# A streaming encoder step on one core: a fixed order for the beginning, token sums in place, the new stream read back from its sum in DRAM, pooling rows on the loads' queue, weight buffers moved

## The chip, the cores and the metric

The kernel runs on one core of a Trainium2 chip, as one launch. The metric is the device time of one execution in microseconds (us); of several runs the median is taken. Engines are named as in the profile: PE (TensorE, matmuls), DVE (VectorE), ACT (ScalarE), POOL (GpSimd, which also issues DMAs through a queue in software), SP (SyncE, which only issues DMAs).

## What is computed

A two-layer trunk over 640 tokens (512 of one prompt, and 8 running streams of 16), width 2048, in float32. Layer A, which the change touches:

```python
h = rmsnorm(x, norm_a[l])
z = h @ w_in_a[l]                       # 2048 -> 2 x 4096
u, gate = z[..., :E_A], z[..., E_A:]
y, st = pool_mix(u, pool_prev[l], pos0, w_grp_a[l], scale_a[l])
x = x + (y * jax.nn.silu(gate)) @ w_out_a[l]
new_pool.append(st)                     # the last 15 rows of u: outputs pool_prompt, pool_sample
```

`pool_mix` takes, for four groups of 1024 channels, the mean over a trailing window of 2, 4, 8 or 16 tokens minus the token, and multiplies each group by its own 1024 x 1024 matrix. Then the stream is normalised and projected once to keys and values (`w_kv`), and layer B attends over them. The outputs are the two streams, K, V, the forget logits and the pooling states.

## The kernel before, in words

Every float32 operand of a product is split into a high part (ACT's rounding copy, names ending in h or hi: `th`, `bh`, `wh`, `whi`) and the rest (a subtraction on DVE: `tl`, `bl`, `wl`, `wlo`), and a product is three matmuls: high by high, high by low, low by high (L242-246). A matmul is 128 x 128 by 128 x 320, since the 640 tokens are handled as two halves.

The large products of layer A are done in pairs, 256 rows by 256 columns at a time, by a scheme with seven products in place of eight (names m1 to m7, `OPER` at L124 says which operands each takes). For it a "side" of two token tiles holds three plain blocks (`bh`, `bl`, L160-163) and four sums of blocks (`th`, `tl`, L165-173). `blocks_t` takes the four sums from the four-block tile `x4` into another tile `t` (L167-170), then splits `t` (L172 on ACT, L173 on DVE). The weights have sums as well (`prep`, L204-226: L209, L212, L213 on DVE, in the last 16 preparations L212 and L213 on POOL; the splits at L86 and L89).

The work runs in this order:

1. The beginning (L322-384): five row tiles of x are loaded, squared (L352), normalised (L361), transposed by PE (L110) and copied into eight tiles `x4s` (L371, L373); from these come the eight sides. PE's first unit (L403) takes m1, m2, m3 of all sides, which need only `bh` and `bl`, and then m5, m6, m7, m4, which need `th` and `tl`.
2. Units u and g (`pair8`, L253): the pooling branch and the gate, 256 channels at a time. A u unit combines its products (L270-291), adds windows on POOL (L463) and stores the differences; its last 15 rows wait in a list of small pieces of work (`pool_rows`, L476), which later units run one at a time (`tick`): PE transposes them (L483), ACT copies them from PSUM (`po`, L485), POOL's queue stores them (L486). The tag `po` has one buffer. The saved states come in through `st` (L423-432).
3. For each of four groups g, four `y_pair` (group matrix, L543; scale and gate on DVE at L562 into `m4`) make the sides `y_[0..3]`, and eight `out_pair` (L567) multiply these by `w_out`, 256 rows of the stream each. In `out_pair` m1, m6, m5, m7 come first; ACT and DVE combine them (L581-585) and POOL's queue adds them to the stream in DRAM (`xacc`, accumulating DMA, L586). Then come m2, m3, m4. In groups 0 to 2 ACT copies these (L599) and two more accumulating DMAs add them (L600, L601). In group 3 SP reads the stream's rows back behind L586 (L589, into `x1`), DVE adds m2, m3, m4 to them (L605), POOL's queue stores the new stream (`xres`, L673), ACT squares it (L638), POOL adds up the squares (L640), and the first eight rows' tiles are split at once, the others later (`late`, L681).
4. The tail: the sum of squares goes to DRAM (`sqd`, L680), the pools of layer A are closed, the K/V weights are loaded into the space (L716), scaled (L722) and split (L730, L732), and PE projects (L701). A matmul with ones (L789) in the first projection, behind its first eight token tiles, sums the squares over partitions.

PE's order is that of the code (`manual_schedule`, L176); the other engines' orders are chosen by the scheduler, which may move an instruction ahead of older ones. DMAs of one queue are issued in order, and an instruction that waits holds up those behind it on its engine or queue. A DMA that writes rows which another DMA is writing waits until that one has landed.

Of the kernel before, what the change touches and what calls it, by code (L numbers as in the profile page):

```python
# [17 lines left out]
P = 128  # L18
# [21 lines left out]
def tile_yoco_step(ctx, tc, i, o):  # L40
# [36 lines left out]
    ident = const.tile([P, P], F32, name="ident")  # L77
    make_identity(nc, ident)
    inv = const.tile([P, 16], F32, name="inv")
    for t in range(16):  # L80
        nc.vector.memset(inv[:, t : t + 1], 1.0 / (t + 1))
# [42 lines left out]
    OPER = {"m1": (0, 0), "m6": (5, 5), "m5": (4, 3), "m7": (3, 4), "m2": (2, 2), "m3": (6, 1), "m4": (1, 6)}  # L124
# [12 lines left out]
    xb_, wa, misc = pool(sa, "xb"), pool(sa, "wa"), pool(sa, "misc")  # L137
# [27 lines left out]
    def blocks_t(sd, x4, t, eng=None):  # L165
        eng = eng or nc.vector
        eng.tensor_tensor(t[:, 0, :], x4[:, 0, :], x4[:, 1, :], op=ALU.subtract)  # L167
        eng.tensor_tensor(t[:, 1, :], x4[:, 2, :], x4[:, 0, :], op=ALU.add)
        eng.tensor_tensor(t[:, 2, :], x4[:, 2, :], t[:, 0, :], op=ALU.add)
        eng.tensor_tensor(t[:, 3, :], x4[:, 3, :], t[:, 2, :], op=ALU.subtract)  # L170
        sd.th, sd.tl = (tslot(sd.j, q, [P, 4, HALF], F32R) for q in "hl")
        nc.scalar.activation(sd.th, t, AF.Copy)  # L172
        nc.vector.tensor_tensor(sd.tl, t, sd.th.bitcast(F32), op=ALU.subtract)  # L173
# [30 lines left out]
    def prep():  # L204
        n = nprep[0]
        raw = loaded.pop(n).rearrange("p (a b) (s n) -> p a (b s) n", a=2, n=P)
        if loads[n][0] == "s":
# [3 lines left out]
            eng = nc.gpsimd if n >= len(loads) - 16 else nc.vector  # L211
            eng.tensor_tensor(sums[:, :, 2, :], sums[:, :, 1, :], raw[:, :, 1, :], op=ALU.add)  # L212
            eng.tensor_tensor(sums[:, :, 3, :], raw[:, :, 3, :], sums[:, :, 2, :], op=ALU.subtract)  # L213
# [56 lines left out]
    cvue = [misc.tile([P, HALF], F32, tag=f"c{q}", name=f"c{q}") for q in "vue"]  # L270
# [47 lines left out]
    gains = [bslot(6 + q // 2, "hl"[q % 2], [P, 512]) for q in range(4)]  # L318
    x4s = [tslot(4 + j // 2, "hl"[j % 2], [P, 4, HALF]) for j in range(8)]
    small = pool(start, "small")  # L320

    idle = small.tile([P, P], F32, name="idle")  # L322
    nc.vector.memset(idle, 0.0)
    for _ in range(8):
        nc.tensor.matmul(banks[:, 7, :P], idle, idle, start=True, stop=True)
# [4 lines left out]
    def half_rows(t):  # L330
# [4 lines left out]
    half_rows(0)  # L335
    for q in range(4):
        dma(gains[q], i["norm_a"][0][q * 512 : (q + 1) * 512].partition_broadcast(P))
# [975 lines left out]
```

## Time and profile before

| | |
|---|---|
| median of 3 runs | 2927.91 us (2926.19 to 2931.11) |
| the profiled execution | 2930.98 us |
| its span, first to last instruction | 2929.3 us |
| mean granted PE clock | 0.981 of full speed |
| PE busy | 2794.5 us, 95% |
| DVE, ACT, POOL busy | 66%, 35%, 13% |
| first unit's last products | until about 104 us |
| u and g units | until about 895 us |
| groups 0 to 3 | 895 to 1577.5 us |
| K/V projection begins | 1600.15 us |

A line of the waits reads "engine tile line <- engine tile line it waited for: us in total, times, longest us". In a timeline, a line has start, length, engine, line, operation, output and inputs; brackets at its end hold the idle time of the engine before it and what ended it. L numbers are lines of the kernel before; the lines of the changed kernel differ by up to some thirty.

### The profile page before, as it was taken

What the parts mean: (1) busy time and instruction counts of PE and PEld (TensorE: products, weight loads), DVE (VectorE), ACT (ScalarE), POOL (GpSimd) and SP (SyncE); (2) the same over time, 40 slices, a digit from 0 to 9 for tenths busy, and PEclk for the clock granted to TensorE, in tenths of its full rate; (3) what the DMA queues carried; (4) which work ended last, traced back from release to release, by engine and by line L of the source; (5) the groups of instructions that cost most, each with busy time, mean ns of one, the idle gap of its engine ahead of it and who ended that gap; (6) DMA issues with size and microseconds to landing.
All of it is one profiled execution on the core that took longest, in us unless ns stands there. A gap on an engine that the chain in (4) does not pass through costs nothing.

```text
span 2929.3 us, 46530 instructions
## 1 busy us (share of the span) xinstructions
PE 2794.5 (95%) x18410; PEld 2691.4 (92%) x18410; DVE 1935.2 (66%) x3350; ACT 1027.0 (35%) x1720; POOL 390.5 (13%) x426
## 2 busy tenths in 40 slices
PE   5899999999999999999986999999999999999998
PEld 4799999989999999999985999999999999999887
DVE  7777877787777848586674755655656666656434
ACT  6333333333334434343332232333333333334222
POOL 1312223133240110202244000000000000000000
PEclk9799999999999999999997999999999999999999
DMA  4344443433435786868466644455544455554823
GB/s 136 98 126 130 132 128 121 134 110 115 131 107 182 182 166 171 170 169 171 121 178 175 163 120 118 115 121 124 131 119 115 119 121 119 120 121 105 148 84 111
DMA packets 677643, 390.36 MB, mean 133 GB/s; under 512 B 323920, under 2 KB 632704, under 8 KB 677296
## 3 DMA queue, kind: packets, MB, share of 16 engines
q1 hardware_dynamic: 652256, 320.61, 41.3%
q0 software_dynamic: 25168, 66.78, 10.4%
q8 instruction: 144, 2.36, 0.3%
q14 instruction: 75, 0.61, 0.1%
HBM read 299.34 MB, written 87.95 MB: 132 GB/s over the span
## 4 chain that ended last, share of the span: by engine, by line
PE 42%; DMA 4%; DVE 1%; SPq 1%; POOL 1%; issue 1%; ACT 0%; DVEq 0%; POOLq 0%; ACTq 0%
PE banks L701 30%; PE banks L1205 5%; PE banks L1133 2%; DMA xacc<-m 2%; PE banks L1034 1%; DMA xt<-xres 1%; PE banks L110 1%; SPq L1243 1%; DMA x<-xacc 1%; POOL bh L640 1%; PE banks L1044 0%; PE banks L1045 0%; PE banks L1046 0%; DVE yn L1246 0%; PE banks L1146 0%
## 5 line engine op out<-in xcount | busy, mean ns | idle before, releaser
L246 PE MATMUL banks<-th,wh 128*128 128x320 f32 x1408 | 447.9, 318 | 12.6 <-ACT th L172 12.2
L246 PE MATMUL banks<-tl,wh 128*128 128x320 f32 x1408 | 442.9, 315 | 17.7 <-DVE tl L173 17.7
L246 PE MATMUL banks<-th,wl 128*128 128x320 f32 x1408 | 441.3, 313 | 0.0
L701 PE MATMUL banks<-th,whi 128*128 128x320 f32 x2048 | 399.6, 317 | 22.7 <-ACT whi L730 22.7
L701 PE MATMUL banks<-tl,whi 128*128 128x320 f32 x2048 | 384.0, 309 | 0.0
L246 PE MATMUL banks<-bh,wh 128*128 128x320 f32 x1056 | 332.8, 315 | 14.8 <-DVE x L605 9.8
L701 PEld LDWEIGHTS banks<-th,whi 128*128 128x128 f32 x2048 | 316.1, 189 | 29.0 <-ACT whi L730 23.0
L246 PE MATMUL banks<-bl,wh 128*128 128x320 f32 x1056 | 331.8, 314 | 3.1 <-DVE bl L163 3.1
L246 PE MATMUL banks<-bh,wl 128*128 128x320 f32 x1056 | 331.6, 314 | 0.6 <-DVE wl L89 0.6
L732 DVE TENSOR_TENSOR wlo<-raw,whi 128x512 fp32r<-128x512 f32 x272 | 186.3, 686 | 212.9 <-ACT whi L730 209.9
L701 PEld LDWEIGHTS banks<-tl,whi 128*128 128x128 f32 x2048 | 321.9, 188 | 0.0
L730 ACT ACTIVATE whi<-raw 128x512 fp32r<-128x512 f32 x272 | 171.7, 632 | 398.6 <-PE banks L701 234.3
L89 DVE TENSOR_TENSOR wl<-raw,wh 128x768 fp32r<-128x768 f32 (+1 forms) x200 | 209.4, 1048 | 142.5 <-ACT wh L86 136.3
L86 ACT ACTIVATE wh<-raw 128x768 fp32r<-128x768 f32 (+1 forms) x200 | 173.5, 869 | 342.8 <-issue 156.0
L246 PEld LDWEIGHTS banks<-tl,wh 128*128 128x128 f32 x1408 | 270.4, 192 | 20.9 <-DVE tl L173 20.9
L246 PEld LDWEIGHTS banks<-th,wh 128*128 128x128 f32 x1408 | 270.5, 192 | 17.2 <-ACT th L172 15.2
L246 PEld LDWEIGHTS banks<-th,wl 128*128 128x128 f32 x1408 | 270.0, 192 | 0.0
L89 DVE TENSOR_TENSOR wl<-sums,wh 128x1024 fp32r<-128x1024 f32 x176 | 223.6, 1271 | 42.5 <-ACT wh L86 41.9
L86 ACT ACTIVATE wh<-sums 128x1024 fp32r<-128x1024 f32 x176 | 185.2, 1052 | 188.6 <-DVE sums L213 183.4
L701 PE MATMUL banks<-th,wlo 128*128 128x320 f32 x1024 | 233.7, 309 | 0.2 <-DVE wlo L732 0.2
L701 PE MATMUL banks<-tl,wlo 128*128 128x320 f32 x1024 | 233.7, 309 | 0.0
L246 PEld LDWEIGHTS banks<-bh,wh 128*128 128x128 f32 x1056 | 203.3, 193 | 16.4 <-DVE x L605 10.3
(376 smaller groups left out, 5156.1 us busy)
## 6 DMA issues: line engine op xcount, KB each, us to landing
raw<-in_w_in_a SPq DMA_DIRECT2D x128, 512.0 KB, 4.0
raw<-in_w_out_a SPq DMA_DIRECT2D x64, 512.0 KB, 4.9
raw<-in_w_kv SPq DMA_DIRECT2D x128, 256.0 KB, 3.1
raw<-in_w_in_b SPq DMA_DIRECT2D x128, 256.0 KB, 3.0
raw<-in_w_grp_a SPq DMA_DIRECT2D x32, 512.0 KB, 5.6
kc<-in_cache_k SPq DMA_DIRECT2D x64, 256.0 KB, 4.1
vc<-in_cache_v SPq DMA_DIRECT2D x16, 1024.0 KB, 7.4
raw<-in_w_out_b SPq DMA_DIRECT2D x64, 256.0 KB, 3.2
```

The lines of the kernel that those rows point to most:

```text
L86: a = nc.scalar.activation(hi, x, AF.Copy)
L89: nc.vector.tensor_tensor(lo, x, hi.bitcast(F32), op=ALU.subtract)
L110: nc.tensor.transpose(out, x, ident[:n, :n])
L246: nc.tensor.matmul(bank[:, :HALF], w[kk][:, a, :], x, start=first and q == 0, stop=last and q == 2)
L640: nc.gpsimd.tensor_tensor(sqs[0], sqs[0], s, op=ALU.add)
L701: nc.tensor.matmul(acc_[:, s, :HALF], w, x[:, s * HALF : (s + 1) * HALF], start=f, stop=l)
L730: nc.scalar.activation(hi, raw, AF.Copy)
L732: nc.vector.tensor_tensor(lo, raw, hi.bitcast(F32), op=ALU.subtract)
L1034: nc.tensor.matmul(sp[rows, b % 2 * PAST : (b % 2 + 1) * PAST], qs[:, rows], kct[:, b * PAST : (b + 1) * PAST], start=True, stop=True)
L1133: nc.tensor.matmul(po[32 * q : 32 * q + 32, :P], pts[:, j, 32 * q : 32 * q + 32], vc[:, 4 * q + j, :], start=(j == 0), stop=False)
L1205: nc.tensor.matmul(out, (ol if q == 2 else oh)[k][:, ts], wl if q == 1 else wh, start=first and q == 0, stop=last and q == 2)
L1243: dma(xt[at].rearrange("p t (j r) -> p t j r", r=32), xres[n * 512 : (n + 1) * 512].rearrange("(j c) (t a r) -> a c t j r", c=32, a=4, r=3 ...
```

## The change

It has five parts.

- **Beginning.** The small row tile (the samples) goes first, the gains come in as single rows and are spread over partitions by PE into PSUM, and DVE, ACT and POOL keep the order of the code from there to the last side's split. The four token sums are formed in place.
- **Token sums in place.** `blocks_t` becomes `sums_t` and `split_t`: the sums overwrite the blocks of `x4` (or of `m4` in `y_pair`), and two rows of `OPER` change with their order.
- **Pooling rows.** `po` has three buffers, which `st` shares; the stores go to SP's queue instead of POOL's.
- **New stream.** In group 3 `out_pair` is as in the other groups: all partial sums are added in DRAM. One pair later POOL's queue reads the finished rows back (`new_stream`), and squares and splits start from these. `xres` is gone; layer B reads `xquad`, of which `xacc` are parts.
- **Buffers.** The pool of layer A's weights (`wa`) is opened before that of the sides (`xb`); two combination buffers become one tile, which also holds the sum of squares; all weight sums are on DVE.

```diff
-    OPER = {"m1": (0, 0), "m6": (5, 5), "m5": (4, 3), "m7": (3, 4), "m2": (2, 2), "m3": (6, 1), "m4": (1, 6)}
+    OPER = {"m1": (0, 0), "m6": (5, 5), "m5": (4, 4), "m7": (3, 3), "m2": (2, 2), "m3": (6, 1), "m4": (1, 6)}
...
-    xb_, wa, misc = pool(sa, "xb"), pool(sa, "wa"), pool(sa, "misc")
+    wa, xb_, misc = pool(sa, "wa"), pool(sa, "xb"), pool(sa, "misc")
...
-    def blocks_t(sd, x4, t, eng=None):
+    def sums_t(x4, eng=None):
+
         eng = eng or nc.vector
-        eng.tensor_tensor(t[:, 0, :], x4[:, 0, :], x4[:, 1, :], op=ALU.subtract)
-        eng.tensor_tensor(t[:, 1, :], x4[:, 2, :], x4[:, 0, :], op=ALU.add)
-        eng.tensor_tensor(t[:, 2, :], x4[:, 2, :], t[:, 0, :], op=ALU.add)
-        eng.tensor_tensor(t[:, 3, :], x4[:, 3, :], t[:, 2, :], op=ALU.subtract)
+        eng.tensor_tensor(x4[:, 1, :], x4[:, 0, :], x4[:, 1, :], op=ALU.subtract)
+        eng.tensor_tensor(x4[:, 0, :], x4[:, 2, :], x4[:, 0, :], op=ALU.add)
+        eng.tensor_tensor(x4[:, 2, :], x4[:, 2, :], x4[:, 1, :], op=ALU.add)
+        eng.tensor_tensor(x4[:, 3, :], x4[:, 3, :], x4[:, 2, :], op=ALU.subtract)
+
+    def split_t(sd, x4):
         sd.th, sd.tl = (tslot(sd.j, q, [P, 4, HALF], F32R) for q in "hl")
-        nc.scalar.activation(sd.th, t, AF.Copy)
-        nc.vector.tensor_tensor(sd.tl, t, sd.th.bitcast(F32), op=ALU.subtract)
+        split(sd.th, sd.tl, x4)
...
-            eng = nc.gpsimd if n >= len(loads) - 16 else nc.vector
-            eng.tensor_tensor(sums[:, :, 2, :], sums[:, :, 1, :], raw[:, :, 1, :], op=ALU.add)
-            eng.tensor_tensor(sums[:, :, 3, :], raw[:, :, 3, :], sums[:, :, 2, :], op=ALU.subtract)
+            nc.vector.tensor_tensor(sums[:, :, 2, :], sums[:, :, 1, :], raw[:, :, 1, :], op=ALU.add)
+            nc.vector.tensor_tensor(sums[:, :, 3, :], raw[:, :, 3, :], sums[:, :, 2, :], op=ALU.subtract)
...
+    steady = ExitStack()
+    steady.enter_context(tc.manual_schedule(engines={mybir.EngineType.DVE, mybir.EngineType.Activation, mybir.EngineType.Pool}))
...
+    order = (4, 0, 1, 2, 3)
+    squares(order[0])
+    for n, t in enumerate(order):
...
     for j in range(8):
         blocks_b(xs_[j], x4s[j])
-        if j in (1, 3, 5):
+        if j in (1, 3):
             prep()
-            for _ in range({1: 1, 3: 0, 5: 3}[j]):
+            if j == 1:
                 fetch()
+        if j in (3, 5, 7):
+            sums_t(x4s[j], nc.gpsimd)
+        if j == 5:
+            sums_t(x4s[0])
     for j in range(8):
-        t = tslot({1: 4, 3: 5, 5: 6}[j], "h", [P, 4, HALF]) if j in (1, 3, 5) else x4slot()
-        blocks_t(xs_[j], x4s[j], t, nc.gpsimd if j % 2 else None)
+        if j + 1 in (1, 2, 4, 6):
+            sums_t(x4s[j + 1])
+        split_t(xs_[j], x4s[j])
+    for _ in range(3):
+        fetch()
+    steady.close()
...
-            po = pu.tile([NB * PAD, P], F32, tag="po", name="po")
+            po = pu.tile([NB * PAD, P], F32, tag="po", name="po", bufs=3)
             nc.scalar.activation(po, tq[: NB * PAD, :P], AF.Copy)
-            store2(o["pool_sample"][0].rearrange("b s e -> (b s) e")[:, c0 + b * P : c0 + (b + 1) * P], po)
+            store(o["pool_sample"][0].rearrange("b s e -> (b s) e")[:, c0 + b * P : c0 + (b + 1) * P], po)
...
         blocks_b(y_[p], m4)
-        blocks_t(y_[p], m4, x4slot())
+        sums_t(m4)
+        split_t(y_[p], m4)
...
-        if x1 is not None:
-            for k in range(2):
-                dma(x1[k], xacc[c][k * P : (k + 1) * P, :])
...
-        else:
-            for m, j in (("m2", 3), ("m3", 2), ("m4", 1)):
-                a = halves(x1[j // 2])[:, j % 2, :]
-                nc.vector.tensor_tensor(a, a, pp[m], op=ALU.add)
+        o3 = bslot(2, "hl"[c % 2 if g < 3 else 0], [P, 3, HALF])
+        for m, j in (("m2", 2), ("m3", 1), ("m4", 0)):
+            nc.scalar.activation(o3[:, j, :], pp[m], AF.Copy)
+        nc.gpsimd.dma_start(xacc[c][:P, HALF:], o3[:, 0, :], accum_op=ALU.add)
+        nc.gpsimd.dma_start(xacc[c][P:, :], o3[:, 1:, :].rearrange("p s n -> p (s n)"), accum_op=ALU.add)
...
+    def new_stream(c):
...
+        for k, x in zip((2 * c, 2 * c + 1), x1):
+            store2(x, xacc[c][k % 2 * P : (k % 2 + 1) * P, :])
+            squares(k, x)
+            if k < 8:
+                split_x(k, x)
+            else:
+                late.append((k, x))
...
             if g < 3:
-                out_pair(g, c)
...
+            elif c:
+                new_stream(c - 1)
         dk = nd
+    new_stream(7)
     store2(sqd, sqs[0])
```

What the scheduler makes of it at two places. First DVE at the end of the last `y_pair` of group 0, where PE is about to need `tl`: `m` is `m4`, `x` the tile `t` of the sums, `draw` are pooled rows for the next group, and L562 (L590 in the changed kernel) writes the last blocks of `m`. Before:

```order
L562 SCALAR_TENSOR_TENSOR m_9205<-banks,cols,sg_9071 128x320 x2
L168 TENSOR_TENSOR x_9340<-m_9205 128x320
L169 TENSOR_TENSOR x_9340<-m_9205,x_9340 128x320
L212 TENSOR_TENSOR sums<-sums,raw 128x2x128
L163 TENSOR_TENSOR bl<-m_9205,bh 128x960
L170 TENSOR_TENSOR x_9340<-m_9205,x_9340 128x320
L213 TENSOR_TENSOR sums<-raw,sums 128x2x128
L89 TENSOR_TENSOR wl<-raw,wh 128x2x384
L89 TENSOR_TENSOR tl<-draw,th 128x1280
L173 TENSOR_TENSOR tl<-x_9340,th 128x1280
```

The same place on DVE after the change, from `bl` on; behind L590 a weight sum (L208) and a weight residual (L84) come first:

```order
L158 TENSOR_TENSOR bl<-m_9230,bh 128x960
L209 TENSOR_TENSOR sums<-raw,sums 128x2x128
L163 TENSOR_TENSOR m_9230<-m_9230 128x320
L164 TENSOR_TENSOR m_9230<-m_9230 128x320
L84 TENSOR_TENSOR tl<-draw,th 128x1280
L165 TENSOR_TENSOR m_9230<-m_9230 128x320
L84 TENSOR_TENSOR wl<-sums,wh 128x2x512
L166 TENSOR_TENSOR m_9230<-m_9230 128x320
L206 TENSOR_TENSOR sums<-raw 128x2x256
L84 TENSOR_TENSOR tl<-draw,th 128x1280
L84 TENSOR_TENSOR tl<-m_9230,th 128x1280
```

Before, three sums precede `bl` and the fourth follows it at once (the first, L167, stood further up). Now all four stand behind `bl`, with a weight residual, a weight sum and two residuals of `draw` among them.

Then POOL's queue in group 3, one pair long. Before (`bh` and `bl` are the read-back rows here, and `bh` also the sum of squares):

```order
L586 DMA xacc_88<-m_14457 128x2x640
L212 TENSOR_TENSOR sums<-sums,raw 128x2x128
L213 TENSOR_TENSOR sums<-raw,sums 128x2x128
L673 DMA xres<-bh 128x640
L640 TENSOR_TENSOR bh<-bh,bl 128x640
L673 DMA xres<-bl 128x640
L640 TENSOR_TENSOR bh<-bh,bl 128x640
L586 DMA xacc_89<-m_14599 128x2x640
```

And now, where L615 is the first accumulation, L626 and L625 the other two, L680 the read-backs and L660 the addition of squares:

```order
L615 DMA xacc_66<-m_14455 128x2x640
L660 TENSOR_TENSOR sq<-sq,bl 128x640
L626 DMA xacc_66<-bh 128x640
L625 DMA xacc_66<-bh 128x320
L680 DMA x_14660<-xacc_66 128x640 x2
L660 TENSOR_TENSOR sq<-sq,bl 128x640
L615 DMA xacc_67<-x_14599 128x2x640
```

The read-backs and the first square of a pair stand ahead of the next pair's first accumulation. On ACT the squares of a pair (L658) stand ahead of the copies of the next pair's m2, m3 and m4:

```order
L610 ACTIVATE m_14734<-banks 128x320
L81 ACTIVATE wh<-sums 128x2x512
L658 ACTIVATE bl<-x_14799 128x640 x2
L624 ACTIVATE bh<-banks 128x320 x2
L81 ACTIVATE bh<-raw 128x384 x2
L81 ACTIVATE bh<-sums 128x512 x2
L624 ACTIVATE bh<-banks 128x320
```

L610 copies m1 of that pair, L624 its m2, m3 and m4, whose banks PE needs again a pair later.

More of the change, by code (lines that the diff above doesn't have):

```diff
@@ L346, in tile_yoco_step @@
[L346 to L353 removed]
+    load_rows(1)
+    load_rows(2)
+    fetch()
+    load_rows(3)
+    fetch()
+    steady = ExitStack()
+    steady.enter_context(tc.manual_schedule(engines={mybir.EngineType.DVE, mybir.EngineType.Activation, mybir.EngineType.Pool}))
```

136 lines of the change are left out of this document (64 added, 72 removed).

## Prediction

> **What bounds the kernel now.** I read the page first, then the waits of TensorE (PE), the windows for the clock, and the timelines around the waits.
>
> ```profile
> span 2929.3 us, 46530 instructions
> ...
> PE 2794.5 (95%) x18410; PEld 2691.4 (92%) x18410; DVE 1935.2 (66%) x3350; ACT 1027.0 (35%) x1720; POOL 390.5 (13%) x426
> ```
>
> PE is busy for 95% of the span, so the change can win only what PE idles (135 us) and what it runs at half clock. Its waits, by whom it waited for:
>
> ```profile
> PE banks L701 <- ACT whi L730: 22.7, 1, 22.7
> PE banks L110 <- ACT po L485: 21.2, 9, 3.4
> PE banks L246 <- DVE tl L173: 17.7, 12, 2.3
> PE banks L246 <- DVE x L605: 14.1, 4, 5.9
> PE banks L246 <- ACT th L172: 12.2, 10, 2.7
> ...
> PE banks L246 <- DVE bl L605: 4.8, 1, 4.8
> ```
>
> Each touched part owns a line: the tail before the K/V projection (22.7), pooling rows (21.2), token sums (17.7 and 12.2), the last group's read-back (14.1 and 4.8). Windows, with the columns stretch, length, busy time of PE, PEld, DVE, ACT, POOL, granted clock, DMA:
>
> ```profile
> 46.00:101.00 55.00, 34.24 (x156) 29.68 (x156) 40.84 (x48) 21.67 (x22) 21.12 (x16) 0.77 0.10 29
> ...
> 1445.60:1577.50 131.90, 110.27 (x675) 107.94 (x673) 79.32 (x113) 46.53 (x67) 60.62 (x63) 0.91 0.56 148
> ```
>
> **The beginning: -9 us.** Between the last row copy and the last token side, DVE is the chain:
>
> ```profile
> 45.70 0.42 DVE L371 COPY tl<-banks 128x256 f32<-128x256 f32 x1 [0.49 <-ACT th L373]
> ...
> 99.48 1.49 DVE L173 TENSOR_TENSOR tl<-x,th 128x1280 fp32r<-128x1280 f32 x1 [2.05 <-ACT th L172]
> ```
>
> From 46.0 to 101.0 DVE works 40.8 us and idles 14.2, mostly for ACT's th as in the last row, which waits for sums on POOL or for the one x4 buffer. In place, no sum waits for that buffer, and the fixed order starts POOL's three sides early. DVE's list after the rows is about as long (five sides' sums instead of four, two weight preparations against parts of three), so I take 40 us. Of the 14 idle us I keep 5: weights whose buffers PE frees late, and DVE's share in the work beside POOL. The rows themselves (other order, gains spread by PE) I put at 47 instead of 46.1, give or take 3. So the last side ends near 92 instead of 101: -9, between -14 and -3. The last matmuls and the state load behind it stay.
>
> **Pooling rows: 0.** The two rows of one pair, with what surrounds them on ACT, DVE and POOL:
>
> ```profile
> 547.14 1.06 ACT L86 ACTIVATE wh<-sums 128x1024 fp32r<-128x1024 f32 x1 [6.69 <-DVE sums L213]
> 548.10 0.26 ACT L485 ACTIVATE po<-banks 120x128 f32<-120x128 f32 x1
> 552.00 0.28 ACT L485 ACTIVATE po<-banks 120x128 f32<-120x128 f32 x1 [3.64 <-DMA out_pool_sample<-po]
> ```
>
> ```profile
> 543.85 1.65 DVE L212 TENSOR_TENSOR sums<-sums,raw 128x256 f32<-128x256 f32 x1
> ...
> 551.04 0.42 DVE L212 TENSOR_TENSOR sums<-sums,raw 128x256 f32<-128x256 f32 x1
> ```
>
> PE's wait is for the first po, and that one stands behind a weight split whose sums DVE finishes late (1.65 against 0.42 us, while POOL adds windows). No store is in that chain; the order on ACT and DVE here is unchanged. What three buffers remove is the second po's wait for the first store (3.64), at which PE does not stand. The stores on SP wait there for ACT's po with weight loads behind them. One load is needed per 42 matmuls, 6.4 us at the page's mean of 2794.5/18410 = 0.152, and three buffers stand ahead: a delay of a microsecond or two is covered; uncovered it would be PE's. Value 0, bounds -21.2 (all of that line, and some 7 us of half clock) and +3.
>
> **Token sums of y: +15.** In place, the first sum overwrites a block that both bh and bl must have read. Before, DVE had three of the four sums done ahead of bl. The last unit of group 0:
>
> ```profile
> 967.35 1.00 DVE L562 SCALAR_TENSOR_TENSOR m<-banks,cols,sg 128x320 f32<-128x320 f32 x2
> ...
> 969.42 1.16 DVE L163 TENSOR_TENSOR bl<-m,bh 128x960 fp32r<-128x960 f32 x1
> 970.50 0.49 DVE L170 TENSOR_TENSOR x<-m,x 128x320 f32<-128x320 f32 x1
> 970.90 0.42 DVE L213 TENSOR_TENSOR sums<-raw,sums 128x256 f32<-128x256 f32 x1
> 971.24 0.95 DVE L89 TENSOR_TENSOR wl<-raw,wh 128x768 fp32r<-128x768 f32 x1
> 972.11 1.48 DVE L89 TENSOR_TENSOR tl<-draw,th 128x1280 fp32r<-128x1280 f32 x1
> 973.51 1.48 DVE L173 TENSOR_TENSOR tl<-x,th 128x1280 fp32r<-128x1280 f32 x1
> 974.91 1.22 DVE L89 TENSOR_TENSOR wl<-sums,wh 128x1024 fp32r<-128x1024 f32 x1
> ```
>
> ```profile
> 972.34 0.41 PE L246 MATMUL banks<-th,wh 128*128 128x320 f32 x1 [0.58 <-ACT th L172]
> 975.05 0.41 PE L246 MATMUL banks<-tl,wh 128*128 128x320 f32 x1 [2.29 <-DVE tl L173]
> ```
>
> DVE has no idle here; from m (968.3) to the end of tl (975.0) are 6.7 us. The new order puts between them, by the starts of these rows: a weight residual 0.87, bl 1.08, a weight sum 0.34, two sums 0.8, a draw residual 1.4, a sum 0.4, a weight residual 1.14, the last sum 0.4, a weight sum 0.6, another draw residual 1.4, tl 1.4, and a weight sum 0.34: 10.2 us. So tl comes 3.5 us later and PE's gap grows from 2.9 to 6.4. Three such places before group 3: +10.5. They also reach half clock:
>
> ```profile
> 972.00:976.00 4.00, 1.36 (x7) 1.14 (x8) 4.00 (x4) 2.84 (x4) 0.00 (x0) 1.00 0.57 174
> ...
> 1133.70:1140.50 6.80, 5.50 (x20) 5.50 (x21) 5.58 (x10) 2.36 (x3) 0.00 (x0) 0.50 0.51 165
> ```
>
> At 972 a gap of 2.9 left the clock at 1.00; at group 1 similar gaps gave 6.8 us at 0.50, worth 3.4. With 6.4 I count one such window more at the other two places, 2 to 3.4 each: about +4.5. [...] Bounds: +3 (DVE's other pieces slip behind) and +22.
>
> **Group 3: +2.** POOL's queue now carries everything of a pair, in order: first accumulation, second and third (they write the same rows, so they wait for the first to land), two read-backs (they wait for both), a square's addition, and only then the next pair's first accumulation. Landing times (us in the last column), here and in group 1:
>
> ```profile
> xacc<-m POOLq DMA_DIRECT2D x8, 640.0 KB, 6.5
> x<-xacc SPq DMA_DIRECT2D x12, 320.0 KB, 3.3
> ```
>
> ```profile
> xacc<-bl POOLq DMA_DIRECT2D x3, 320.0 KB, 4.7
> xacc<-bh POOLq DMA_DIRECT2D x3, 320.0 KB, 6.2
> ```
>
> ```profile
> L640 POOL TENSOR_TENSOR bh<-bh,bl x15: 1538/1573/1981, 1473.3 to 1589.7; 128x640 f32<-128x640 f32 x15
> ```
>
> ```profile
> L638 ACT ACTIVATE bl<-x x11: 736/737/742, 1471.2 to 1573.7; 128x640 f32<-128x640 f32 x11
> ```
>
> ```profile
> 1459.55 1.24 POOL L586 DMA_DIRECT2D xacc<-m  x1 [4.00 <-issue]
> ...
> 1576.04 1.24 POOL L586 DMA_DIRECT2D xacc<-m  x1
> ```
>
> 6.5 + 5.5 + 3.3 + 0.74 + 1.57 and 1.1 for issuing make 18.7 us a pair, against (1576.0 - 1459.6)/7 = 16.6 now; 84 matmuls at 0.152 need 12.8. PE follows the chain one pair behind, since ACT's copies of m2, m3, m4 stand behind squares that wait for the read-back. That slack returns most: the first accumulation goes at 1461 (this group's own sums are 1.7 late), the seventh at 1573.3, and PE's last matmul 6.4 later, at 1579.7 instead of 1577.5. The additions on DVE and the stores of the residual stream go, but neither is then what PE waits for. Bounds: -27 (PE at its own pace) and +14 (21 us a pair). [...]
>
> **The tail: +9.** Now:
>
> ```profile
> 1591.91 2.92 DMA sqd<-bh
> ...
> 1609.87 1.08 PE banks L789 x4
> ```
>
> ```profile
> 1600.15 1.43 PE L701 MATMUL banks<-th,whi 128*128 128x320 f32 x4 [22.69 <-ACT whi L730]
> ```
>
> PE idles from 1577.5 to 1600.2 because the K/V weights' buffers lie where the squares' sum is read until it is stored. Moved, the weights come early; but ACT still has the last pairs' copies, squares and splits before the first whi, and I put the restart at 21 us behind the last matmul instead of 22.7. The sum of squares needs the last pair: its first accumulation at 1592, then 6.5 + 5.5 + 3.3, squares and additions 3.9, the store 2.9, the load (a read-back's size) 3.3: about 1618, 38.5 behind PE's last matmul. The norm matmul that needs it stands in PE's order after eight k, 32.4 behind it now. So PE stalls a second time: +6, and +3 for half clock after it. Bounds -20 (both stalls gone) and +14.
>
> Everything else (preparations moved from POOL to DVE, merged buffers, the stream reread from another tensor of the same size) hides under DVE's 53 idle us of group 3 or the B layer: 0.
>
> **Sum.** -9 + 0 + 15 + 2 + 9 = +17: 2948 for the profiled execution of 2931.0, which is 3.1 above the median of 2927.9; against the median, 2945. About 0.2% (6 us) is what a measurement of this kernel can tell from no change.
>
> **Rivals.**
> - *Read-back hidden* (faster): DRAM traffic without the residual stores lands faster or is waited for two pairs behind, PE keeps 12.8 us a pair, and the 18.9 us of waits for L605 go with their half clock (0.91 over that window). -27 instead of +2: 2916. It decides where the chain falls below some 14 us; against it stands the sum of 18.7, for it that no matmul reads the new stream.
> - *Pooling rows were the stores' fault* (faster): -28 instead of 0, 2917. Against it: the first po, not the second, is what PE stands at.
> - *The sums cost nothing* (same): DVE's foreign pieces wait for their own inputs and tl goes early: 0 instead of +15, 2930.
> - *Longer chain* (slower): 21 us a pair, +14: 2959.
>
> **Numbers.** Forecast 0.50, longer chain 0.10, sums free 0.10, read-back hidden 0.15, pooling 0.11, both of these together (2888) 0.04. Faster by over 0.2%: 0.30. Within: 0.14 (sums free, and the forecast's lower edge). Slower: 0.56. The forecast alone spans 2932 to 2958; the range takes in either gain and the longer chain, 2900 to 2966.
>
> **What would show it.** First unit's last matmul near 95 instead of 104; PE gaps of 6 us before each group's first output pair; first accumulations of group 3 spaced 18 to 19 us; a second stall of 7 to 10 us before the ones-matmul of the norm; unchanged waits for po. Spacing of 13 us, no stall at the norm, or a vanished po line would make it wrong.

## The result, and the profile after

The changed kernel takes 2974.88 us (median of 4 runs, 2973.32 to 2977.27), beside 2928.14 for the kernel before in 4 runs on the same chip: a ratio of 1.0159 (1.0142 to 1.0177), 46.7 us slower. The forecast was 2945 with a range up to 2966: the sign was right, the size fell outside. The profiled execution took 2974.87 us with a span of 2973.0, 43.7 longer than before.

The page of the changed kernel, its span and the engines' busy times:

```profile
span 2973.0 us, 46467 instructions
...
PE 2811.3 (95%) x18418; PEld 2702.5 (91%) x18418; DVE 1943.2 (65%) x3358; ACT 1037.4 (35%) x1744; POOL 337.1 (11%) x342
```

PE's busy time grew by 17 of the 44 us. Seven of the 17 are the eight matmuls that spread the gains (L353, from 6.1 to 13.3 us); the other ten come with the lower clock (0.970 granted on average, 0.981 before), since the products are the same. The other 27 us are waits. Who is waited for (the lines of `th`, `tl` and `bh` answer to L172, L173 and L605 of before, L725 to L701, L105 to L110):

```profile
PE banks L242 <- ACT th L81: 20.5, 4, 5.9
...
PE banks L725 <- ACT whi L754: 20.2, 1, 20.2
...
PE banks L105 <- ACT po L513: 19.2, 8, 3.3
PE banks L242 <- ACT bh L624: 16.1, 5, 7.8
...
PE banks L813 <- DMA sq<-sqd: 11.7, 1, 11.7
```

The wait for token sums now comes four times at up to 5.9 us, where the longest was 2.7; the wait for `po` stays; the wait for the read-back has become one for ACT's copies (L624); and a second stall stands in the tail (L813).

Where the 43.7 us came, by the starts of PE's matmuls in both traces:

| stretch | before | after | predicted | measured |
|---|---|---|---|---|
| start to u unit 1 | 106.65 | 107.89 | -9 | +1.2 |
| units, to the first `y_pair` of group 0 | 803.8 | 801.8 | 0 | -2.0 |
| groups 0 to 2 | 479.0 | 493.4 | +15 | +14.4 |
| group 3, to the end of PE's last output matmul | 188.0 | 204.4 | +2 | +16.4 |
| past the first 96 matmuls of the projection | 40.4 | 51.2 | +9 | +10.8 |
| the rest | | | 0 | +2.9 |

In the kernel before, the units end at 910.4 us and not at about 895. Three of the five terms hold within 2 us (pooling rows, whose place is the units, token sums and the tail); two are off by 10 and 14, both the same way. The lines behind them follow. First POOL's queue over one pair of group 3 (L615 first accumulation, L626 and L625 the other two, L680 read-back, L660 a square's addition):

```profile
1577.26 1.26 POOL L615 DMA_DIRECT2D xacc<-m  x1
1578.17 1.94 POOL L660 TENSOR_TENSOR sq<-sq,bl 128x640 f32<-128x640 f32 x1
1585.21 0.93 POOL L626 DMA_DIRECT2D xacc<-bh  x1 [5.11 <-issue]
1585.82 1.20 POOL L625 DMA_DIRECT2D xacc<-bh  x1
1592.89 0.57 POOL L680 DMA_DIRECT2D bl<-xacc  x1 [5.87 <-DMA xacc<-bh]
1594.60 0.57 POOL L680 DMA_DIRECT2D bh<-xacc  x1 [1.14 <-DMA xacc<-bh]
1598.70 1.53 POOL L660 TENSOR_TENSOR sq<-sq,bl 128x640 f32<-128x640 f32 x1 [3.52 <-ACT bl L658]
1600.17 1.25 POOL L615 DMA_DIRECT2D xacc<-x  x1
```

Each entry waits for the one ahead: 7.9 us from the first accumulation to the second, 9.4 to the last read-back, 5.6 to the next pair; at 22.9 us this pair is a long one. The first and the last L615 of the group, from the same view:

```profile
1476.36 1.21 POOL L615 DMA_DIRECT2D xacc<-x  x1 [56.53 <-issue]
...
1619.23 1.24 POOL L615 DMA_DIRECT2D xacc<-m  x1
```

Seven spacings in 142.9 us: 20.4 a pair, against 16.6 before. Second, DVE and PE at the end of the last `y_pair` of group 0, the place shown in order above. DVE, with the last `m` at 967.6 and `tl` done at 978.8:

```profile
966.60 1.00 DVE L590 SCALAR_TENSOR_TENSOR m<-banks,cols,sg 128x320 f32<-128x320 f32 x2
...
968.72 1.15 DVE L158 TENSOR_TENSOR bl<-m,bh 128x960 fp32r<-128x960 f32 x1
...
972.01 1.49 DVE L84 TENSOR_TENSOR tl<-draw,th 128x1280 fp32r<-128x1280 f32 x1 [0.87 <-ACT th L81]
...
975.96 1.48 DVE L84 TENSOR_TENSOR tl<-draw,th 128x1280 fp32r<-128x1280 f32 x1
977.36 1.48 DVE L84 TENSOR_TENSOR tl<-m,th 128x1280 fp32r<-128x1280 f32 x1
```

PE, the same microseconds:

```profile
976.80 0.63 PE L242 MATMUL banks<-th,wh 128*128 128x320 f32 x1 [5.74 <-ACT th L81]
...
978.90 0.64 PE L242 MATMUL banks<-tl,wh 128*128 128x320 f32 x1 [1.47 <-DVE tl L84]
```

From `m` to `tl` are 11.2 us (10.2 predicted), and PE's gap is 7.2 us where it was 2.9. Third, the two stalls of the tail on PE:

```profile
1627.74 1.44 PE L725 MATMUL banks<-th,whi 128*128 128x320 f32 x4 [20.22 <-ACT whi L754]
...
1648.69 2.47 PE L813 MATMUL banks<-sq,ones 128*128 128x320 f32 x4 [11.71 <-DMA sq<-sqd]
```

And the beginning in windows, first of before, then of after (columns as in the prediction):

```profile
0.00:42.00 42.00, 18.59 (x81) 16.81 (x82) 29.40 (x94) 30.34 (x78) 0.70 (x6) 1.00 0.62 213
52.00:106.00 54.00, 32.79 (x147) 27.82 (x145) 38.34 (x50) 15.97 (x16) 21.34 (x18) 0.75 0.13 34
```

```profile
0.00:42.00 42.00, 25.06 (x88) 18.26 (x88) 22.74 (x73) 26.61 (x73) 0.70 (x6) 0.75 0.51 175
...
52.00:106.00 54.00, 36.54 (x168) 32.87 (x167) 51.82 (x61) 24.53 (x26) 12.98 (x14) 0.78 0.13 38
```

DVE did 29.4 us of work in the first 42, now 22.7, and idles for the other 19; what it did not do then it does behind the rows, where it is busy for 51.8 of 54 us. Three weight preparations begin on DVE in these 42 us before (L209 at 14.9, 28.3 and 37.7), two now (L206 at 30.5 and 41.1). (PE's longer busy time there is the eight matmuls that spread the gains, 7.2 us.)

### The profile page after: what moved, and what is told of

Its sections match the earlier page's. It is cut to its first block, busy times and chain, and to the rows that moved or that the text cites. A ratio compares the mean times of both kernels' runs of the same rounds, so it can differ in the third digit from the quotient of the medians.

```text
span 2973.0 us, 46467 instructions
## 1 busy us (share of the span) xinstructions
PE 2811.3 (95%) x18418; PEld 2702.5 (91%) x18418; DVE 1943.2 (65%) x3358; ACT 1037.4 (35%) x1744; POOL 337.1 (11%) x342
## 3 DMA queue, kind: packets, MB, share of 16 engines
q1 hardware_dynamic: 656824, 316.54, 40.4%
q0 software_dynamic: 25424, 68.50, 11.2%
## 4 chain that ended last, share of the span: by engine, by line
PE 41%; DMA 4%; issue 1%; DVE 1%; SPq 1%; POOL 1%; ACT 1%; DVEq 0%; ACTq 0%; POOLq 0%
PE banks L725 30%; PE banks L1229 4%; PE banks L1157 2%; DMA xacc<-bh 1%; PE banks L1058 1%; DMA xt<-xacc 1%; PE banks L105 1%; SPq L1267 1%; DMA x<-xacc 1%; DMA raw<-in_w_out_b 0%; DMA xacc<-m 0%; POOL sq L660 0%; PE banks L242 0%; PE banks L1068 0%; DVE yn L1270 0%
## 5 line engine op out<-in xcount | busy, mean ns | idle before, releaser
L242 PE MATMUL banks<-th,wh 128*128 128x320 f32 x1408 | 447.0, 317 | 20.7 <-ACT th L81 20.5
L725 PE MATMUL banks<-th,whi 128*128 128x320 f32 x2048 | 400.5, 317 | 20.2 <-ACT whi L754 20.2
L725 PE MATMUL banks<-tl,whi 128*128 128x320 f32 x2048 | 384.0, 309 | 0.0
L725 PEld LDWEIGHTS banks<-th,whi 128*128 128x128 f32 x2048 | 316.7, 189 | 26.7 <-ACT whi L754 20.5
L725 PEld LDWEIGHTS banks<-tl,whi 128*128 128x128 f32 x2048 | 322.0, 188 | 0.0
L84 DVE TENSOR_TENSOR wl<-raw,wh 128x768 fp32r<-128x768 f32 (+1 forms) x200 | 209.5, 1049 | 147.1 <-ACT wh L81 147.0
L242 PEld LDWEIGHTS banks<-th,wh 128*128 128x128 f32 x1408 | 270.6, 192 | 22.7 <-ACT th L81 21.5
L84 DVE TENSOR_TENSOR wl<-sums,wh 128x1024 fp32r<-128x1024 f32 x176 | 223.7, 1271 | 47.7 <-ACT wh L81 47.0
L725 PE MATMUL banks<-th,wlo 128*128 128x320 f32 x1024 | 233.8, 310 | 0.0
L725 PE MATMUL banks<-tl,wlo 128*128 128x320 f32 x1024 | 233.7, 309 | 0.0
```

The costliest lines, as they stand in the source:

```text
L84: nc.vector.tensor_tensor(lo, x, hi.bitcast(F32), op=ALU.subtract)
L242: nc.tensor.matmul(bank[:, :HALF], w[kk][:, a, :], x, start=first and q == 0, stop=last and q == 2)
L725: nc.tensor.matmul(acc_[:, s, :HALF], w, x[:, s * HALF : (s + 1) * HALF], start=f, stop=l)
```

## Experiments

Two theories stood after this. For the beginning: the sums in place gain what was predicted and the fixed order takes it back (against: the sums in place bring nothing there, or POOL's sums cost it). For group 3: the chain in POOL's queue is longer than the sum (against: the accumulations themselves became slow, or the earlier waits only add up). Times are medians; each kernel ran beside the kernel before, whose medians were 2927.9 to 2930.9, so kernels of different comparisons are set against each other by their ratios. "Marks" are starts of PE's matmuls as in the table.

**Single parts, each alone in the kernel before.**

e1_sums: the token sums of y in place; the beginning keeps its own tile.

```diff
...
         blocks_b(y_[p], m4)
-        blocks_t(y_[p], m4, x4slot())
+        sums_t(m4)
+        split_t(y_[p], m4)
```

> The kernel before with one part alone: the token sums of y formed in place (the beginning keeps its separate tiles). If the parts of the loss are local and add up, this gives +12 to +16 us, with PE gaps of 6 to 7 us ahead of the first output pair of groups 0, 1 and 2 and nothing new elsewhere. Rival: the gaps come from other moves of the scheduler that the whole change brings, then it is within 4 us of before.

Measured: 2952.74, ratio 1.0086 (1.007 to 1.0103), +25 by the runs, more than expected. Its profiled execution lies only 17 above: it is the fastest of the four (2948.58 to 2956.81) and has the highest granted clock, 0.977 against 0.969 to 0.973 in the others. PE, at the same place:

```profile
975.07 0.64 PE L256 MATMUL banks<-th,wh 128*128 128x320 f32 x1 [5.18 <-ACT th L86]
...
977.17 0.63 PE L256 MATMUL banks<-tl,wh 128*128 128x320 f32 x1 [1.47 <-DVE tl L89]
```

The gap is 6.65, and the marks of groups 1, 2 and 3 are 3.5, 6.7 and 12.9 late. Groups 0 to 2 take 493.7 us, as in the changed kernel: this part alone makes their loss.

e2_stream: the new stream read back from DRAM on POOL's queue, alone. The merged combination buffers and the weight sums on DVE come with it.

```diff
...
+        for k, x in zip((2 * c, 2 * c + 1), x1):
+            store2(x, xacc[c][k % 2 * P : (k % 2 + 1) * P, :])
...
+            elif c:
+                new_stream(c - 1)
...
```

> The kernel before with one part alone: all partial sums of group 3 added in DRAM and read back one pair later on POOL's queue. If POOL's in-order chain sets the pace, first accumulations of group 3 stand about 20.4 us apart, PE's last output matmul comes 14 to 18 us later than before, and, since the K/V weights still wait for the store of the squares, PE restarts about 45 us behind that matmul instead of 23: +35 to +42 us in all. Rival: group 3 was slow in the changed kernel through the sums in place or the moved buffers, then the spacing stays below 18 us and the loss is under +25.

Measured: 2958.1, 1.0099 (1.0084 to 1.0114), +29. Its first accumulations are 20.5 us apart ((1599.34 - 1456.14)/7), the last output matmul comes 9 late (14 to 18 were expected), and the weights, here still in the old buffers, come later too:

```profile
PE banks L696 <- ACT whi L725: 42.9, 1, 42.9
```

So the slow chain needs none of the other parts, and no late sums.

e3_wa: the weights' pool ahead of the sides', alone.

```diff
-    xb_, wa, misc = pool(sa, "xb"), pool(sa, "wa"), pool(sa, "misc")
+    wa, xb_, misc = pool(sa, "wa"), pool(sa, "xb"), pool(sa, "misc")
```

> The kernel before with one part alone: the pool of layer A's weights opened ahead of that of the sides. If the K/V weights wait for the store of the squares only because of where they lie, PE restarts 12 to 14 us behind the last output matmul instead of 22.7 and the ones-matmul finds its input: -7 to -10 us. Rival: ACT's and DVE's late splits or the loads themselves set the restart, then -3 to 0.

Measured: 2923.62, 0.9983 (0.9973 to 0.9992), -5. In its trace the stall before the projection is 15.8 instead of 22.7 and the projection starts 9.9 us earlier, but 1000 matmuls later 4.7 are left. In between a new wait of 2.9 us stands at L878 (for the load of `cl`), one at L1044 is 0.6 longer, and PE is busy for 1.8 us more (granted clock 0.99 against 1.00): together the 5.3 that the lead lost.

e4_begin: the fixed beginning, sums in place there, y's sums in their own tile. Its diff is the beginning's part of the one above.

> The kernel before with one part alone: the beginning in a fixed order with its sums in place. By the marks of the two traces +1 to +2 us (row tiles end 5 us later, the sides then catch up 4). Rival, the prediction's: the late end in the whole change came from other parts (buffers that lie elsewhere), then alone it is -9 to -4.

Measured: 2929.41, 1.0003 (0.9994 to 1.0012): nothing. Unit 1 starts at 105.55 (106.65 before).

e5_pool: pooling rows with three buffers on SP's queue, alone.

```diff
...
-            po = pu.tile([NB * PAD, P], F32, tag="po", name="po")
+            po = pu.tile([NB * PAD, P], F32, tag="po", name="po", bufs=3)
...
-            store2(o["pool_sample"][0].rearrange("b s e -> (b s) e")[:, c0 + b * P : c0 + (b + 1) * P], po)
+            store(o["pool_sample"][0].rearrange("b s e -> (b s) e")[:, c0 + b * P : c0 + (b + 1) * P], po)
```

> The kernel before with one part alone: pooling rows in three buffers, stored from SP's queue. PE waits for the first row of a pair, which stands behind a weight split on ACT, not behind a store: the line of PE's waits for po stays at 18 to 22 us, and the time is 0 to -3 us. Rival: the stores were the cause; the line falls below 8 us and the time by 20 us or more.

Measured: 2933.19, 1.0005 (0.9997 to 1.0014). The wait is what it was:

```profile
PE banks L110 <- ACT po L487: 20.4, 8, 3.4
```

In this trace each of the eight `po` that PE waits for follows on ACT right behind the split of a weight sum, which itself had waited 4.6 to 6.8 us for DVE.

The five parts alone sum to about +52 (25 + 29 - 5 + 1 + 1.5) against +46.7 together.

**The chain of group 3, loosened step by step in the changed kernel.**

e6_readsp: the read-backs go to SP's queue.

```diff
-            store2(x, xacc[c][k % 2 * P : (k % 2 + 1) * P, :])
+            dma(x, xacc[c][k % 2 * P : (k % 2 + 1) * P, :])
```

> The changed kernel with the read-backs of group 3 issued by SP in place of POOL; the squares are still added on POOL, ahead of the next pair's first accumulation. If the chain over the squares sets the pace, only the issue on POOL goes: first accumulations 19 to 20 us apart, -3 to -10 us against the changed kernel. Rival: the transfers' place on POOL's queue is the cost: 13 to 15 us apart, -30 or more.

e7_spread: e6, and DVE adds the squares.

```diff
-            nc.gpsimd.tensor_tensor(sqs[0], sqs[0], s, op=ALU.add)
+            nc.vector.tensor_tensor(sqs[0], sqs[0], s, op=ALU.add)
```

> The changed kernel with the read-backs issued by SP and the squares added on DVE, so that POOL's queue holds only accumulations and none waits for a read-back. If the in-order chain is what paces group 3, first accumulations come 13 to 15 us apart and PE's last output matmul 35 to 45 us earlier than in the changed kernel. Rival: accumulation in DRAM itself is too slow (6.5 and then 6.1 us), or the copies on ACT behind the squares hold PE: 18 us apart or more, -10 us or less.

e9_pin: e7, and on ACT a pair's copies of m2, m3, m4 and the squares keep the order of the code, so the squares stand behind the next pair's copies.

```diff
-            nc.scalar.activation(o3[:, j, :], pp[m], AF.Copy)
+            a3 = nc.scalar.activation(o3[:, j, :], pp[m], AF.Copy)
+            if g == 3:
+                tc.keep_in_program_order(a3)
...
-        nc.scalar.activation(s, x, AF.Square)
+        tc.keep_in_program_order(nc.scalar.activation(s, x, AF.Square))
```

> The changed kernel with SP's read-backs and DVE's additions as in the run before, and on ACT the squares of a pair held behind the copies of the next pair's m2, m3 and m4. With POOL's queue free the spacing was 17.4 us; if what was left of the chain is ACT's copies behind squares that wait for a read-back, the spacing falls to 13 to 14.5 us and PE's last output matmul comes 15 to 25 us earlier than in that run. Rival: the transfers themselves (14 us for a pair's accumulations) hold it: 16.5 to 17.5 us still.

| | time | ratio (interval) | us a pair | last output matmul |
|---|---|---|---|---|
| changed kernel | 2974.88 | 1.0159 (1.0142 to 1.0177) | 20.4 | 1607.5 |
| e6_readsp | 2965.34 | 1.0117 (1.01 to 1.0134) | 18.9 | 1599.0 |
| e7_spread | 2955.96 | 1.0082 (1.0067 to 1.0097) | 17.4 | 1587.8 |
| e9_pin | 2939.86 | 1.0036 (1.0024 to 1.0047) | 14.7 | 1578.8 |

Each step takes a link out of the chain and the spacing falls by 1.5, 1.5 and 2.7. e7 was expected to gain twice as much; POOL's timeline of e7 shows what held it instead:

```profile
1599.25 1.20 POOL L615 DMA_DIRECT2D xacc<-m  x1 [11.21 <-ACT bh L624]
```

and ACT's of e7 in the same place, where the copies (L624) stand behind two squares (L658), and these behind the read-back:

```profile
1596.22 0.74 ACT L658 ACTIVATE bl<-x 128x640 f32<-128x640 f32 x1 [13.26 <-DMA x<-xacc]
1597.85 0.74 ACT L658 ACTIVATE bl<-x 128x640 f32<-128x640 f32 x1 [0.89 <-DVE sq L660]
1598.50 0.75 ACT L624 ACTIVATE bh<-banks 128x320 f32<-128x320 f32 x2
```

The chain had a second way round, through ACT. e9 cuts it: in its ACT timeline the copies go first and the square of the pair before comes 5.7 us behind them.

```profile
1568.22 1.09 ACT L624 ACTIVATE bh<-banks 128x320 f32<-128x320 f32 x3 [5.59 <-DMA xacc<-bh]
1573.95 0.74 ACT L660 ACTIVATE bl<-bh 128x640 f32<-128x640 f32 x1 [4.63 <-DMA bh<-xacc]
```

With it, three accumulations and a read-back of every row cost no more than the old stores did (14.7 us a pair, 16.6 before). That decides against slow accumulations: the first one lands later in e9 than in the changed kernel (8.2 to 8.7 us against 6.5 and 6.6) and the pairs are still 5.7 us closer.

**The beginning.**

e11_free: e4 without the fixed order.

```diff
-    steady.enter_context(tc.manual_schedule(engines={mybir.EngineType.DVE, mybir.EngineType.Activation, mybir.EngineType.Pool}))
```

> The beginning alone, as in the fourth run, but with the scheduler choosing the order on DVE, ACT and POOL. If the fixed order costs (two weight preparations inside the row tiles, 4.2 us each), row tiles end 4 to 6 us earlier than in that run and the first unit 4 to 8 us earlier. Rival: the sums beside POOL and the chain through ACT set the end: within 2 us of that run.

Measured: 2914.55, 0.9947 (0.9932 to 0.9962), -15.5; unit 1 starts at 91.21. Its window, to be read beside that of the changed kernel above:

```profile
0.00:42.00 42.00, 25.34 (x103) 19.90 (x104) 30.26 (x92) 30.95 (x84) 0.70 (x6) 0.69 0.61 201
52.00:91.00 39.00, 27.51 (x132) 24.71 (x132) 38.07 (x49) 15.93 (x16) 10.07 (x11) 0.78 0.13 35
```

and e4's, with the order fixed:

```profile
0.00:42.00 42.00, 23.26 (x88) 17.70 (x88) 24.04 (x75) 27.15 (x74) 0.70 (x6) 0.76 0.51 175
```

With the scheduler's order DVE does 6.2 us more in the same 42, and 38 are left behind the rows. So the new beginning without its fixed order is worth 15.5 us, and the order takes all of it. Which of its other edits (sums in place, order of the row tiles, gains spread by PE) brings how much of the 15.5 wasn't separated.

e12_nopool: e4 with all sums on DVE.

```diff
-            sums_t(x4s[j], nc.gpsimd)
+            sums_t(x4s[j])
```

> The beginning alone in its fixed order, with all token sums on DVE. DVE gets 12 sums more (0.4 us each, 4.8) and loses what POOL beside it stretches (about 8 us between 60 and 81): first unit's end 2 to 4 us earlier than in the fourth run. Rival: DVE is the chain and POOL's help is worth its price: 3 to 5 us later.

Measured: 2930.97, 1.001 (1.0 to 1.0019); unit 1 at 107.98, 2.4 later than in e4. The times of e4 and e12 are within each other's intervals, so POOL's sums are not the loss; that they help rests on this mark alone.

e16_afree: the whole change, only its fixed order taken out (the edit of e11).

> The changed kernel whole, with the order of its beginning left to the scheduler. If the fixed order is the one thing that spoils the beginning, it is 13 to 17 us faster than the changed kernel: 2957 to 2963 us. Rival: later parts of the change wait for something else (group 3's chain starts from weights, not from the start) and take part of it back: 2966 to 2975.

Measured: 2965.22, 1.0122 (1.0105 to 1.0139), some 11 less than the whole by the ratios, between the two ranges that were stated. In its trace unit 1 starts 13.2 us ahead of before (the changed kernel: 1.2 behind); some of that lead over the changed kernel is lost in the groups and the tail, for reasons that weren't followed, and its span, 2964.4, is 8.6 shorter.

**The token sums of y.**

e8_sums3: e1, but the last `y_pair` of each group has its own tile.

```diff
...
+        if p == 3:
+            blocks_t(y_[p], m4, x4slot())
+        else:
+            sums_t(m4)
+            split_t(y_[p], m4)
```

> The kernel before with the sums of y in place in the first three units of each group, and in a tile of their own in the last one. If the loss of the sums lies only where PE needs them at once, at the end of each group's last unit, nothing is left: -3 to +3 us against the kernel before. Rival: sums in place cost in each unit, through the one buffer of m that is held longer: +10 us or more.

Measured: 2933.98, 1.0014 (1.0005 to 1.0023), +4. PE, at the place shown for e1:

```profile
970.09 0.41 PE L256 MATMUL banks<-th,wh 128*128 128x320 f32 x1 [0.71 <-ACT th L86]
...
971.61 0.63 PE L256 MATMUL banks<-tl,wh 128*128 128x320 f32 x1 [1.11 <-DVE tl L89]
```

Three of four sides may be summed in place for some 4 us; the one that PE waits for costs some 20 us (1.0086 against 1.0014).

e15_sumspin: e1, with the splits of `draw` and of the sums held in the order of the code on ACT and DVE, so that none of `draw` stands ahead of `tl`.

```diff
...
-        split(dk[-1][0], dk[-1][1], raw)
+        tc.keep_in_program_order(nc.scalar.activation(dk[-1][0], raw, AF.Copy))
+        tc.keep_in_program_order(nc.vector.tensor_tensor(dk[-1][1], raw, dk[-1][0].bitcast(F32), op=ALU.subtract))
...
```

> The sums of y in place as in the first run, but the splits of the pooled rows for the next group kept behind the last unit's own split, on ACT and DVE. If the foreign residuals of 1.4 us between the sums are the cost, DVE needs about 7.4 us from m to the end of tl (6.7 before, 10.2 with them): the loss of +25 in the first run falls to 0 to +7. Rival: overwriting m itself costs (the sums behind bl, m4's buffer): +12 or more stays.

Measured: 2958.47, 1.0103 (1.0088 to 1.0118). The gap falls to 4.2 us, in PE's timeline of e15:

```profile
983.20 0.64 PE L256 MATMUL banks<-th,wh 128*128 128x320 f32 x1 [3.31 <-ACT th L579]
...
984.72 0.64 PE L256 MATMUL banks<-tl,wh 128*128 128x320 f32 x1 [0.89 <-DVE tl L580]
```

but the four `y_pair` of group 0 take 63.95 us instead of 56.3: PE now waits for the pinned splits of `draw` (2.6 us idle, none before) and runs at a granted 0.92 instead of 1.00. Of the 3.8 us by which e1 widened this gap, 2.4 would thus be the foreign residuals and the rest the overwriting. The gap of group 1 agrees (7.2 in e1, 4.4 here); that of group 2, with new waits for `bh` and `bl`, is no shorter (7.1 against 6.6). For the time the run decides nothing.

**Together.**

e10_wpin: the kernel before with the weights' pool moved and the stream as in e9. e14_best2: e11 and the weights' pool. e13_best: e11, the weights' pool and the stream as in e9; y's sums and pooling rows as before. The new line against e11, in e13 and e14, is that of e3; the rest are the edits of e6, e7 and e9.

> The kernel before (its beginning, sums in their own tile, its pooling rows) with the weights' pool moved and the new stream from DRAM in the mended form: read-backs on SP, additions on DVE, squares behind the copies. If the causes found so far are all, group 3 runs near PE's pace and nothing stalls at the norm: 2890 to 2915 us. Rival: group 3 has a floor elsewhere (weight loads behind the read-backs on SP), then 2920 to 2935.

> The beginning as in the eleventh run and the weights' pool moved, nothing else. Independent parts: -15.5 and -5, so 2905 to 2912 us, and group 3 as before. Rival: as for the run before.

> Beginning with its sums in place but the order left to the scheduler, sums of y in a tile of their own, weights' pool moved, new stream from DRAM with read-backs on SP, additions on DVE and squares behind the copies. If the parts are independent, the gains of the tenth and eleventh run add: -15.5 and -10.5, so 2900 to 2907 us. Rival: an earlier beginning is eaten by weight loads further on, then 2912 to 2920.

Measured: e10 2919.12, 0.9964 (0.995 to 0.9978), between the range that was expected and its rival's; e14 2912.59, 0.9944 (0.9928 to 0.996), 4 less gain than the sum of its parts; e13 2905.25, 0.9917 (0.9902 to 0.9932), 24.3 us faster than the kernel before and 70 faster than the changed one. e13's pairs are 14.8 us apart ((1546.18 - 1442.39)/7). What is left there in the tail, by PE's timeline of e13:

```profile
1578.88 2.47 PE L819 MATMUL banks<-sq,ones 128*128 128x320 f32 x4 [7.28 <-DMA sq<-sqd]
```

## Why the prediction was wrong in size

**The beginning failed: -9 predicted, +1.2 measured.** The steps were "The rows themselves (other order, gains spread by PE) I put at 47" and "DVE's list after the rows is about as long". Rows end at 51.6, and the list took 50.9 us instead of 45. DVE was busy for 49.1 of them, with 55 instructions, and idle for 1.9: the work was put too low, at 40, and not the idle time. The list holds 20 small sums on DVE instead of 15, five of which took over 1 us beside POOL's, and 8 weight residuals instead of 6 (the two preparations that were counted have 4). The gain of the other edits was there, and larger than priced (-15.5 in e11); the fixed order took it back. What the prediction took for a help, POOL's three sides, is worth 2.4 us by one mark (e12). The prediction read DVE's window from 46 on only, and not the one ahead of it, with 94 DVE instructions in 42 us: there the scheduler had filled the waits of the row tiles with weight preparations; a fixed list leaves those waits empty, as the changed kernel's 19 idle us show beside 12.6 before, and runs the preparations in one piece, between row tiles or behind them.

**Pooling rows, 0: right** (e5), and for its reason: PE stands at the first `po`, behind a split of weights, in all eight waits of that trace.

**Token sums of y, +15: right in sum (+14.4), by some luck in its parts.** The gaps for `th` and `tl` grew by 4.3, 4.4 and 4.1 us, 12.9 in all instead of 10.5; at the first of them DVE also waited 0.87 for `th` of `draw`. Over groups 0 to 2 PE idles 11.9 us more (9.7 before, 21.6 now; a wait of 1.0 for `bh` and `bl` went), and its busy time grew by 2.6 for the same products, with a granted clock of 0.98 instead of 0.99, less than the 4.5 predicted. Gaps too small and half clock too large nearly cancel. The 3.4 us for a window of 6.8 at half clock was too much already: PE was busy for 5.5 us in it and can have lost half of that. The windows around the three gaps in the changed kernel, with the granted clock third from the end:

```profile
974.00:980.00 6.00, 1.73 (x5) 1.39 (x6) 5.55 (x7) 2.95 (x3) 0.00 (x0) 0.50 0.64 179
...
1139.00:1147.00 8.00, 3.61 (x12) 3.26 (x13) 7.88 (x11) 3.41 (x3) 0.00 (x0) 0.59 0.57 174
...
1304.00:1312.00 8.00, 4.51 (x18) 4.17 (x19) 7.20 (x11) 2.54 (x2) 0.00 (x0) 0.57 0.54 167
```

All three fell to half clock, but PE ran little in them, and the half clock that before had at the second place (1133.7) was there already. The 3.41 us just ahead of the half clock, at the first place in the changed kernel and then at the second in before:

```profile
969.81:973.22 3.41, 1.24 (x9) 0.98 (x7) 2.50 (x5) 2.52 (x4) 0.00 (x0) 1.00 0.92 280
```

```profile
1130.34:1133.75 3.41, 1.41 (x6) 0.93 (x6) 3.41 (x6) 2.96 (x4) 0.00 (x0) 1.00 0.51 184
```

PE idles 2.2 and 2.0 us in them, and the clock fell behind both. The 3.41 us ahead of the half clock at the second and the third gap hold no PE at all (1137.06 to 1140.47 and 1300.90 to 1304.31, PE busy for 0.00 us), but the first gap runs from 971.06 to 976.80 and the clock fell at 973.22, 2.2 us into it, and the half clock at 1133.7 came behind gaps of 0.24, 0.78 and 0.71 and the first 1.0 of one of 2.29. So in these traces it also fell behind steps that were idle only in part; the last section has the count.

**Group 3 failed in size: +2 predicted, +16.4 measured.** The mechanism, an in-order chain with PE one pair behind, held, and the rival "longer chain" is what came. The term is the sum "6.5 + 5.5 + 3.3 + 0.74 + 1.57 and 1.1". Over the seven spacings the links measure: from the first accumulation to the second 7.3 (6.5 predicted), on to the second read-back 7.2 (5.5), on to the next pair 5.9 (5.6 and the issues 1.1): 20.4 for 18.7. The 5.5 was a mean of two landing times; the last one counts, and it is that of the smaller transfer, issued 0.6 later. This is the list of landing times in the changed kernel:

```profile
xacc<-bh POOLq DMA_DIRECT2D x8, 320.0 KB, 5.2
xacc<-m POOLq DMA_DIRECT2D x4, 640.0 KB, 6.6
...
xacc<-bh POOLq DMA_DIRECT2D x8, 160.0 KB, 6.1
```

Counted from the start of group 3, the first accumulation goes at 73.2 (71.6 predicted), the seventh at 197.0 (183.9), the last matmul 7.4 behind it (6.4): 1.6 + 11.5 + 1.0 = 14 us, the whole error. The chance of 0.10 for the longer chain was too small: a sum of six terms that leaves out every wait between them has its errors on one side, and each tenth of a microsecond counted six times on the way from the first pair to the seventh. By the same sum 21 us a pair would have been +16, as its 2959 has it, and not the +14 of its bound.

**The tail, +9: right (+10.8).** The first stall is 20.2 (21 predicted), the ones-matmul runs 41.2 behind the last output matmul (38.5), and the second stall is 11.7 (7 to 10). The part that moves the weights gains alone (-5, e3); the longer chain takes it back.

**The rest, +2.9,** lies mostly in layer B and wasn't followed up. The rivals "read-back hidden", "pooling rows" and "the sums cost nothing" fell to e2, e5 and e1. "Read-back hidden" becomes true once the chain is cut in both places (e9, 14.7 us a pair).

## What to carry to other kernels

Follow one round through every in-order queue that it touches: an accumulation, its read-back, a reduction of what was read and the next accumulation on one queue ran one behind the other (20.4 us a pair here, 14.7 with the chain cut in e9), and a copy that frees PE's banks must not stand behind work that waits for that read-back. Before an order is fixed by hand, count how many foreign instructions the scheduler had put into its waits, and put as many there. Working in place costs little where the consumer is far off (4 us in e8), and a reordering where it is next (25 us in e1): change only the buffers that nobody waits for.

## What the runs showed of the hardware

- Of two accumulating transfers from one queue, issued 0.6 us apart, the smaller landed later: 160 KB in 6.1 us and 320 KB in 5.2. With the read-backs on SP's queue (e6) they took 5.0 and 4.5; the read-backs themselves did not become faster by that, 3.4 us from POOL and 4.1 from SP for the tiles named `x`. For those named `bl` it is 3.2 and 2.9.
- In the beginning of the changed kernel DVE's small sums ran slower beside POOL's: the same sum takes

```profile
69.56 1.15 DVE L164 TENSOR_TENSOR th<-th 128x320 f32<-128x320 f32 x1
...
970.64 0.49 DVE L164 TENSOR_TENSOR m<-m 128x320 f32<-128x320 f32 x1
```

  with POOL adding at 69 us and idle at 970. Of the 84 sums of this kind in that trace, the 77 with POOL idle take 0.48 to 0.50 us, and of the seven that overlap POOL's five take 1.04 to 1.15. In e12, where POOL adds nothing in the beginning, all of these sums take 0.48 or 0.49 us.

- In the traces of before and of the changed kernel the granted clock changes only at steps of 3.41 us. It fell to half 14 and 22 times, always behind a step in which PE idled for at least 1.86 us; behind no step with more than 1.90 us of idle time did it stay full. It rose again only behind steps with at most 0.52 us idle; behind those with 0.55 or more it stayed at half. (Idle time is what PE's rows leave free; their ends are modelled.)
